# Query and key splits for two heads at once, copied into place by transfers, with weighed blocks evacuated first and projections reordered

## The chip, the cores and the metric

The kernel runs on one core of one Trainium2 chip. The metric is the device time of one execution in microseconds, as the median of several runs.

## What is computed

Two layers of a decoder trunk over 528 positions (16 learned meta tokens and 512 real ones) of width 1024, in float32. Each layer has a mixer and a ConvGLU feed-forward network (FFN), both between two RMS norms. The mixer reads one combined projection of the normed input and feeds three groups, whose outputs are normed by heads, concatenated and projected back:

```python
q, k, v, f_logit, a_val, a_gate, sc_b, sc_c, sc_x = jnp.split(z, idx, axis=-1)
log_f = jax.nn.log_sigmoid((f_logit + b_forget).astype(jnp.float32))
y_attn = forgetting_attention(q.reshape(hs), k.reshape(hs), v.reshape(hs), log_f)
...
a = a_val * jax.nn.sigmoid(a_gate)
a = causal_depthwise_conv(a, a_dw_w) + a_dw_b
a = jax.nn.silu(layer_norm(a, a_ln_g, a_ln_b))
y_conv = jnp.einsum("blc,ce->ble", a, a_pw_w)
y_sc = sc_b * causal_depthwise_conv(sc_c * sc_x, sc_conv_w)
y = jnp.concatenate([y_attn, y_conv, y_sc], axis=-1)
y = jnp.einsum("ble,ed->bld", head_rms_norm(y, head_g), w_out)
return h + rms_norm(y, post_g)
```

The attention has 8 heads of 64. A logit is q·k/8 + F[t] − F[s], causal, with F the running sum of the log forget gates; a softmax over s follows.

## The kernel before

**Layout and precision.** The sequence lies along the free axis (528 positions, two halves of 264), channels on the 128 partitions. Each float32 operand of a large product is split into a high part, rounded to the fast format fp32r, and a low part, the rest; a product is three passes, high·high, high·low, low·high (`mm3`, L639 to L652). So TensorE gets 3 passes x 8 channel blocks x 2 halves = 48 products of 264 columns for each projection of 128 output channels.

**Weights.** A weight block of 128 x 1024 is loaded by SyncE into one of three `raw` buffers (L615), cast to its high part by ScalarE (L619) and its low part taken by VectorE (L623).

**The mixer.** `mixer_steps` lists the projections. Those of the conv module's gate and of the first short-conv group come first; the others run as one thread, `fill`, in the order of the list: v and q, k for pairs of heads (j = 0 to 3), the second short-conv group (sc_c, sc_x, sc_b with j = 1), and `pw`, at which the conv module's tail starts as a thread (`conv_tail`: mean at L1539, variance at L1568, SiLU by Exp and Ln, pointwise product, head norm). Beside `fill` run `maxima`, `exponentials` and `att_norms`.

- `q_proj` and `k_proj` (L1290 and following) project two heads at once into a PSUM bank and split them: for each head and half, ScalarE writes the high part (L1298, L1326) and VectorE the low part (L1303, L1331), 64 partitions each. A head has four tiles, k1, k2, q1 and q2: k1 and q1 hold the high parts on the head's 64 rows and gate and maximum on the other rows; q2 holds q's low part on the other rows and k2 its own low part, and one transfer each (L530, tiles `q<-q` and `k<-k`) copies the high part beside it. There are four such sets of tiles, so heads 4 to 7 reuse those of heads 0 to 3.
- `maxima` (L1372) multiplies q1 by k1 by blocks of queries to find each row's maximum (VectorE, L1379), puts the maxima on a diagonal (GpSimd, L1387) and spreads them by a product (L1396) into a row of q1 (ScalarE, L1398).
- `exponentials` multiplies two pairs of tiles into transposed logits (`logits`, L1416), which ScalarE exponentiates (`pf`, L1423) and GpSimd masks on diagonal blocks (L1430); two blocks later `weigh` multiplies them by the values (L1450) into `acc`, for which there is one PSUM bank. When a query range is summed, ScalarE squares it into `sq` (L1463) and copies it to `yta` (L1464); only then is the bank free.
- `att_norms` norms a pair of heads (L1516) through `head_norm` (L1100 to L1124), which writes `yhi` and `ylo` for the output projection.

When `maxima` and `fill` are over, the output projection of the first half may start on the channel blocks that are normed (`Early`), and on the second half when `exponentials` is over.

**What sets the order.** For ScalarE, VectorE, GpSimd and TensorE, the order is that in which a planner (`Flow`) emits the instructions. Every step is given an engine, a cost in us (`act_us`, `dve_us`, `stt_us`), the tokens that it waits for and a priority; of the steps that are ready, that with the lowest number goes first. Threads (generators) issue TensorE's products and give way to each other where they yield a token. Each engine then runs its instructions in this order. The transfers on SyncE's queue are put in order by the framework, by the tiles that they depend on, and run in that order too.

The gate's rows are spread by ten small transfers (`k<-sq` eight times, `g_dram<-sq` twice, L530), for heads 4 to 7 by two each later (`k<-g_dram`).

## Time and profile before

| | us |
|---|---|
| median of three runs | 1313.34 (1311.2 to 1314.71) |
| the profiled execution | 1311.54 |
| its span, first to last instruction | 1309.8 |
| TensorE busy in the span | 1282.9 |
| VectorE, ScalarE, GpSimd busy | 865.1, 621.2, 97.7 |
| mean granted TensorE clock | 0.996 |

In the profile, PE is TensorE's products, PEld its weight loads, DVE VectorE, ACT ScalarE, POOL GpSimd and SP SyncE; L12 is line 12 of the kernel. A busy PE is not PE at its peak: products are pipelined, and their ends are modelled. A group of instructions is named by its line and by what it writes and reads, `out<-in`. A line of the waits says who waited for whom, with us in total, times, and the longest; in a timeline, a bracket gives the idle time before an instruction and what ended it.

### The profile page before, as it was taken

How to read it: one execution, taken by the hardware profiler on the slowest of the kernel's cores; microseconds unless marked ns; L12 is line 12 of the kernel's file. 1: busy time of each engine (PE TensorE's matmuls, PEld its weight loads, DVE VectorE, ACT ScalarE, POOL GpSimd, SP SyncE). 2: the span in 40 equal slices, each digit the busy share in tenths (PEclk: the TensorE clock that was granted, in tenths of full speed). 3: DMA queues.
4: the chain of work that ended last, by engine and by line, in shares of the span. 5: the costliest groups of instructions: out<-in, count | busy, mean ns of one | idle time of the engine just before them, and what ended most of it. 6: DMA issues, size and time to landing. Idle time of an engine off the chain costs nothing. (4 is left out here: it accounts for less than half of the span.)

```text
span 1309.8 us, 23934 instructions
## 1 busy us (share of the span) xinstructions
PE 1282.9 (98%) x9802; PEld 1228.0 (94%) x9802; DVE 865.1 (66%) x1473; ACT 621.2 (47%) x1167; POOL 97.7 (7%) x254
## 2 busy tenths in 40 slices
PE   8999999999999999999989999999999999999997
PEld 8989898999999999999989898889999799989997
DVE  7888865688634663566676888656876246646664
ACT  7255567564423342344662556675643233314353
POOL 1322311000000000000003223110000000000000
PEclk9999999999999999999989999999999999999999
DMA  6133111602222223223340332125032233233321
GB/s 236 34 99 89 60 58 50 223 20 85 94 95 83 98 72 106 91 85 99 108 137 18 99 90 71 47 74 200 17 97 97 85 94 95 71 110 96 92 71 65
DMA packets 42797, 118.26 MB, mean 90 GB/s; under 512 B 4848, under 2 KB 15216, under 8 KB 42688
## 3 DMA queue, kind: packets, MB, share of 16 engines
q1 hardware_dynamic: 42640, 116.61, 28.0%
q8 instruction: 77, 1.26, 0.4%
q14 instruction: 32, 0.26, 0.1%
q0 software_dynamic: 48, 0.13, 0.0%
HBM read 108.04 MB, written 4.33 MB: 86 GB/s over the span
## 5 line engine op out<-in xcount | busy, mean ns | idle before, releaser
L650 PE MATMUL psum<-uhi,whi 128*128 128x264 f32 (+1 forms) x1936 | 451.5, 287 | 1.9 <-ACT uhi L831 1.1
L650 PE MATMUL psum<-ulo,whi 128*128 128x264 f32 (+1 forms) x1936 | 446.7, 285 | 0.5 <-DVE ulo L1827 0.4
L650 PE MATMUL psum<-uhi,wlo 128*128 128x264 f32 (+1 forms) x1936 | 444.8, 284 | 0.0
L650 PEld LDWEIGHTS psum<-uhi,whi 128*128 128x128 f32 x1936 | 322.9, 189 | 5.8 <-issue 2.4
L650 PEld LDWEIGHTS psum<-ulo,whi 128*128 128x128 f32 x1936 | 323.8, 189 | 1.4 <-DVE ulo L1827 0.6
L650 PEld LDWEIGHTS psum<-uhi,wlo 128*128 128x128 f32 x1936 | 323.7, 189 | 0.0
L650 PE MATMUL psum<-yhi,whi 128*128 128x264 f32 (+3 forms) x888 | 249.6, 304 | 1.5 <-ACT yp L1978 1.0
L650 PE MATMUL psum<-ylo,whi 128*128 128x264 f32 (+3 forms) x888 | 245.6, 299 | 1.0 <-DVE ylo L1124 0.8
L650 PE MATMUL psum<-yhi,wlo 128*128 128x264 f32 (+3 forms) x888 | 245.5, 299 | 1.0 <-DVE wlo L623 0.9
L505 ACT CAST whi<-raw 128x1024 fp32r<-128x1024 f32 (+1 forms) x110 | 113.3, 1031 | 213.0 <-PE psum L650 199.4
L506 DVE TENSOR_TENSOR wlo<-raw,whi 128x1024 fp32r<-128x1024 f32 (+1 forms) x110 | 131.9, 1200 | 81.6 <-ACT whi L505 79.5
L650 PEld LDWEIGHTS psum<-yhi,whi 128*128 128x128 f32 x888 | 159.1, 188 | 10.1 <-ACT yp L1978 1.4
L650 PEld LDWEIGHTS psum<-ylo,whi 128*128 128x128 f32 x888 | 159.3, 188 | 7.6 <-DVE ylo L1124 2.0
L650 PEld LDWEIGHTS psum<-yhi,wlo 128*128 128x128 f32 x888 | 159.1, 188 | 7.2 <-DVE wlo L623 1.8
L1927 DVE SCALAR_TENSOR_TENSOR c<-z,pv,c 128x528 f32<-128x528 f32 (+1 forms) x176 | 132.0, 756 | 2.7
L623 DVE TENSOR_TENSOR wlo<-raw,whi 128x1024 fp32r<-128x1024 f32 (+2 forms) x86 | 102.4, 1205 | 36.6 <-ACT whi L619 35.9
L619 ACT CAST whi<-raw 128x1024 fp32r<-128x1024 f32 (+2 forms) x86 | 87.7, 1033 | 32.4 <-DMA raw<-in_w_dram 17.3
L966 DVE SCALAR_TENSOR_TENSOR cacc<-apad,pv,cacc 128x528 f32<-128x528 f32 x120 | 87.7, 772 | 0.5
L1945 ACT CAST yhi<-c 128x528 fp32r<-128x528 f32 (+1 forms) x44 | 27.6, 627 | 111.3 <-DVE c L1941 111.3
L1937 ACT ACTIVATE c<-c 128x528 f32<-128x528 f32 (+1 forms) x44 | 28.1, 639 | 81.7 <-DVE c L1927 81.7
L1890 DVE TENSOR_TENSOR z<-psum,rz 128x528 f32<-128x528 f32 x40 | 28.3, 708 | 53.8 <-PE psum L650 52.2
L1925 ACT ACTIVATE c<-z,pv 128x528 f32<-128x528 f32 (+1 forms) x88 | 63.3, 726 | 0.0
(212 smaller groups left out, 1438.2 us busy)
## 6 DMA issues: line engine op xcount, KB each, us to landing
raw<-in_w_dram SPq DMA_DIRECT2D x160, 512.0 KB
raw<-in_w_dram SPq DMA_DIRECT2D x32, 448.0 KB
h<-in_x_dram SPq DMA_DIRECT2D x16, 264.0 KB
raw<-in_w_dram SPq DMA_DIRECT2D x4, 528.0 KB
q<-q SPq DMA_DIRECT2D x16, 132.0 KB
k<-k SPq DMA_DIRECT2D x16, 132.0 KB
h_dram<-h SPq DMA_DIRECT2D x4, 528.0 KB
h<-h_dram SPq DMA_DIRECT2D x8, 264.0 KB
```

The source lines that it names most:

```text
L505: nc.scalar.copy(hi[:, :sz], raw[:, :sz])
L506: nc.vector.tensor_sub(lo[:, :sz], raw[:, :sz], hi[:, :sz].bitcast(F32))
L619: nc.scalar.copy(box["hi"][:, :sz], box["raw"][:, :sz])
L623: nc.vector.tensor_sub(lo[:, :sz], box["raw"][:, :sz], box["hi"][:, :sz].bitcast(F32))
L650: nc.tensor.matmul(d, lhsT=w[a][:, k, cols], rhs=rhs(b, k, hf), start=start and i == 0 and p == 0, stop=stop and i == n - 1 and p == 2)
L966: nc.vector.scalar_tensor_tensor(conv[j], in0=src, in1=conv[j], scalar=col("a_dw_w", CK * j + i), op0=ALU.mult, op1=ALU.add)
L1890: nc.vector.tensor_mul(two(t[:, off:]), srcs[0], two(rz))
L1925: nc.scalar.activation(dst, src[:, 2:2 + 2 * fw], AF.Copy, scale=wtap(2, t))
L1927: nc.vector.scalar_tensor_tensor(dst, in0=src[:, i:i + 2 * fw], scalar=wtap(i, t), in1=dst, op0=ALU.mult, op1=ALU.add)
L1937: silu = nc.scalar.activation(cs[0], cs[0], AF.Silu)
L1945: nc.scalar.copy(ghi, cs[0])
```

## The change

There are three parts.

1. `mixer_steps`: `v` with j = 1 goes ahead of the third pair's q and k, `pw` ahead of the fourth pair's; the second short-conv group comes last.
2. `q_proj` and `k_proj`: the high part of both heads is written by one ScalarE step per half, over 128 partitions, into a tile `pair_hi`, and the low part by one VectorE step into `pair_lo` (two buffers each, `NPAIR`). Transfers on SyncE's queue then copy 64 partitions each into the heads' tiles: for q, the high part to q1 and q2 and the low part to q2; for k, the high part to k1 and k2 and the low part to k2. That is three per head and tensor, where there was one. The maxima now wait for transfers of q and k.
3. `weigh`: both evacuations get priority 0 (1 before). The tokens that the square waits for are now those of the last pair's norm product (`norm_mm`) and no longer those of the whole norm (`norm_at`).

```diff
 def mixer_steps():
-    return [("sc_c", 0), ("sc_x", 0), ("v", 0), ("q", 0), ("k", 0), ("sc_b", 0), ("q", 1), ("k", 1), ("q", 2),
-            ("k", 2), ("v", 1), ("q", 3), ("k", 3), ("sc_c", 1), ("pw", 0), ("sc_x", 1), ("sc_b", 1)]
+    return [("sc_c", 0), ("sc_x", 0), ("v", 0), ("q", 0), ("k", 0), ("sc_b", 0), ("q", 1),
+            ("k", 1), ("v", 1), ("q", 2), ("k", 2), ("pw", 0), ("q", 3), ("k", 3), ("sc_c", 1), ("sc_x", 1), ("sc_b", 1)]
...
+            yield from proj(split_pair(j, DH ** -0.5, q_pair))
+            for hd in (2 * j, 2 * j + 1):
                 main, other, _ = rows(hd)
                 q1, q2 = qh[hd % 4]
+                q_at[hd] = [part(q_pair[j], "hi", q1, main, main), *([zeros[hd]] if hd in zeros else [])]
+                q2_at[hd] = [part(q_pair[j], "lo", q2, other, main), part(q_pair[j], "hi", q2, main, main)]
+            q_pair[j]["slot"].close()
+
+        q_pair, k_pair, pair_ring = {}, {}, Ring(NPAIR)
+
+        def part(box, name, t, to, main):
+            tok = flow.op("sp", 0.48, lambda: nc.sync.dma_start(t[to].bitcast(F32), box[name][main].bitcast(F32)),
+                          box[name, "at"], lat=2.2)
+            box["slot"].use(tok)
+            return tok
+
+        def split_pair(j, scale, pairs):
+            box = pairs[j] = {"slot": Slot(), ("hi", "at"): [], ("lo", "at"): []}
             def use(hf, ps, tok):
...
+                    nc.scalar.activation(box["hi"][:, c], ps, AF.Copy, scale=scale)
...
+                    nc.vector.scalar_tensor_tensor(box["lo"][:, c], in0=ps, scalar=scale, in1=box["hi"][:, c].bitcast(F32),
+                                                   op0=ALU.mult, op1=ALU.subtract)
+                a = act(act_us(H), high, tok, *box["hi", "at"], prio=0, takes=() if hf else [(pair_ring, box["slot"])])
+                d = dve(stt_us(H), low, a, prio=0)
...
         def k_proj(j):
...
+            yield from proj(split_pair(j, 1.0, k_pair))
             for hd in (2 * j, 2 * j + 1):
                 main, other, _ = rows(hd)
                 k1, k2 = kh[hd % 4]
-                q2_at[hd].append(dma(k2[other].bitcast(F32), k1[main].bitcast(F32), *k_at[hd], lat=2.2))
+                k_at[hd] = [part(k_pair[j], "hi", k1, main, main)]
+                q2_at[hd] += [k_at[hd][0], part(k_pair[j], "lo", k2, main, main), part(k_pair[j], "hi", k2, other, main)]
...
-                waits = norm_at.get(pr - 1 if e == 0 else None, [zero]) + norm_at.get(pr - 1, [zero])
+                waits = norm_mm.get(pr - 1, [zero])
                 n = qz - qa
-                a = act(act_us(n), lambda: nc.scalar.activation(sq[:, qa:qz], acc[:, :n], AF.Square), tok, *waits)
-                c = act(act_us(n), lambda: nc.scalar.copy(yt[r, qa:qz], acc[r, :n]), tok)
+                a = act(act_us(n), lambda: nc.scalar.activation(sq[:, qa:qz], acc[:, :n], AF.Square), tok, *waits, prio=0)
+                c = act(act_us(n), lambda: nc.scalar.copy(yt[r, qa:qz], acc[r, :n]), tok, prio=0)
```

More of the change, by code (lines that the diff above doesn't have):

```diff
@@ L50 @@
 NP = 6
+NPAIR = 2
 WARM, WARM_US = 44, 8.0
@@ L1294, in q_proj @@
                      for hd in (2 * j, 2 * j + 1)} if j > 1 else {}
-            def high(hd, c, ps):
-                main = rows(hd)[0]
-                nc.scalar.activation(qh[hd % 4][0][main, c], ps[main], AF.Copy, scale=DH ** -0.5)
-            def low(hd, c, ps):
+            yield from proj(split_pair(j, DH ** -0.5, q_pair))
+            for hd in (2 * j, 2 * j + 1):
                 main, other, _ = rows(hd)
                 q1, q2 = qh[hd % 4]
-                nc.vector.scalar_tensor_tensor(q2[other, c], in0=ps[main], scalar=DH ** -0.5,
-                                               in1=q1[main, c].bitcast(F32), op0=ALU.mult, op1=ALU.subtract)
@@ L1306, in use @@
-            def use(hf, ps, tok):
-                out = []
-                for hd in (2 * j, 2 * j + 1):
-                    c = half_sl(hf)
-                    a = act(act_us(H), lambda hd=hd: high(hd, c, ps), tok, prio=0)
-                    d = dve(dve_us(H), lambda hd=hd: low(hd, c, ps), a, prio=0)
-                    q_at.setdefault(hd, [zeros[hd]] if hd in zeros else []).append(a)
-                    q2_at.setdefault(hd, []).append(d)
-                    out += [a, d]
-                return out
@@ L1317, in q_proj @@
-            yield from proj(use)
-            for hd in (2 * j, 2 * j + 1):
-                main = rows(hd)[0]
-                q1, q2 = qh[hd % 4]
-                q2_at[hd].append(dma(q2[main].bitcast(F32), q1[main].bitcast(F32), *q_at[hd], lat=2.2))
-        def k_proj(j):
-            def high(hd, c, ps):
-                main = rows(hd)[0]
-                nc.scalar.copy(kh[hd % 4][0][main, c], ps[main])
-            def low(hd, c, ps):
-                main = rows(hd)[0]
-                k1, k2 = kh[hd % 4]
-                nc.vector.tensor_sub(k2[main, c], ps[main], k1[main, c].bitcast(F32))
-            def use(hf, ps, tok):
-                out = []
-                for hd in (2 * j, 2 * j + 1):
-                    c = half_sl(hf)
-                    a = act(act_us(H), lambda hd=hd: high(hd, c, ps), tok, prio=0)
-                    d = dve(dve_us(H), lambda hd=hd: low(hd, c, ps), a, prio=0)
-                    q2_at[hd] += [a, d]
-                    if hf == 0:
-                        k_at[hd, 0] = a
-                    else:
-                        k_at[hd] = [k_at[hd, 0], a]
-                    out += [a, d]
-                return out
-            yield from proj(use)
@@ new lines, in split_pair, with high, low @@
+        def split_pair(j, scale, pairs):
+            box = pairs[j] = {"slot": Slot(), ("hi", "at"): [], ("lo", "at"): []}
+            def use(hf, ps, tok):
+                c = half_sl(hf)
+                def high():
+                    if hf == 0:
+                        box["hi"], box["lo"] = (T(ap, [P, L], F32R, f"pair_{n}", NPAIR) for n in ("hi", "lo"))
+                    nc.scalar.activation(box["hi"][:, c], ps, AF.Copy, scale=scale)
+                def low():
+                    nc.vector.scalar_tensor_tensor(box["lo"][:, c], in0=ps, scalar=scale, in1=box["hi"][:, c].bitcast(F32),
+                                                   op0=ALU.mult, op1=ALU.subtract)
+                a = act(act_us(H), high, tok, *box["hi", "at"], prio=0, takes=() if hf else [(pair_ring, box["slot"])])
+                d = dve(stt_us(H), low, a, prio=0)
+                box["hi", "at"].append(a)
+                box["lo", "at"].append(d)
+                return [a, d]
+            return use
@@ L1350, in k_proj @@
                 k1, k2 = kh[hd % 4]
-                q2_at[hd].append(dma(k2[other].bitcast(F32), k1[main].bitcast(F32), *k_at[hd], lat=2.2))
+                k_at[hd] = [part(k_pair[j], "hi", k1, main, main)]
+                q2_at[hd] += [k_at[hd][0], part(k_pair[j], "lo", k2, main, main), part(k_pair[j], "hi", k2, other, main)]
                 if j > 1:
                     gate_rows(hd, *g_done)
+            k_pair[j]["slot"].close()
             k2_at[j] = True
```

## The prediction

> **What bounds the kernel now.** I began with the page: which engine is busy, and whether any other comes near it. Then one table of stages, to see where TensorE stands still; then the waits of its weight loads, the first thing of a product to be held up; then single stretches.

> ```profile
> span 1309.8 us, 23934 instructions
> PE 1282.9 (98%) x9802; PEld 1228.0 (94%) x9802; DVE 865.1 (66%) x1473; ACT 621.2 (47%) x1167; POOL 97.7 (7%) x254
> ```

> ```profile
> core 0: us, PE busy (x) PEld busy (x) DVE busy (x) ACT busy (x) POOL busy (x), PEclk, DMA share, GB/s
> 60.00:100.00 40.00, 38.75 (x294) 35.90 (x293) 35.82 (x85) 20.01 (x51) 7.15 (x16) 1.00 0.29 82
> 180.00:220.00 40.00, 37.81 (x262) 33.30 (x261) 25.91 (x67) 32.79 (x92) 6.09 (x19) 1.00 0.12 41
> 350.00:400.00 50.00, 50.00 (x412) 50.00 (x411) 17.88 (x20) 14.72 (x20) 0.00 (x0) 1.00 0.28 96
> 840.00:880.00 40.00, 37.25 (x261) 32.57 (x260) 26.04 (x59) 33.74 (x94) 3.75 (x9) 1.00 0.10 29
> ```

> TensorE is busy 98% of the span, and the change adds or removes no product, so it can only win time in which TensorE waits. The table says where: in the FFN (350 to 400) it never stops, and 50 us / 412 gives 0.121 us for one projection product of 264 columns. The mixers run from about 45 to 230 and from 695 to 885. Their ends (180 to 220, 840 to 880) lose 2.2 and 2.75 us of 40, and there ScalarE is at its fullest, 32.8 and 33.7 us of 40. The waits of the weight loads name the culprits:

> ```profile
> PEld psum L1450 <- POOL pf L1430: 5.6, 8, 1.4
> ...
> PEld psum L1450 <- ACT sq L1463: 2.2, 2, 1.1
> PEld psum L650 <- DVE ylo L1124: 2.0, 5, 0.5
> PEld psum L650 <- DVE wlo L623: 1.8, 4, 0.6
> ...
> PEld psum L1264 <- DVE gt L1256: 1.8, 2, 0.9
> ...
> PEld psum L650 <- ACT yhi L1123: 0.9, 4, 0.3
> ```

> The columns are us in total, times, longest. The weighing product (L1450, weights times values) waits 5.6 + 2.2 = 7.8 us in the two layers, 3.9 us in each. The first products of the output projection wait for their normed input (L1123 and L1124) 2.0 + 0.9 = 2.9 us, and for weight pieces (L623) 1.8. The forget gate's 1.8 (L1264) isn't touched. All that the change can reach is thus 7.8 + 2.9 + 1.8 = 12.5 us, 1.0% of the span. This caps the gain.

> What do the two longest waits look like? ScalarE, GpSimd and TensorE late in the first mixer:

> ```profile
> 195.73 0.72 ACT L1560 CAST yhi<-cacc 128x264 fp32r<-128x264 f32 x2
> 196.34 0.43 ACT L1557 ACTIVATE apad<-apad 128x264 f32<-128x264 f32 x1
> 196.67 0.27 ACT L1463 ACTIVATE sq<-psum 128x128 f32<-128x128 f32 x1
> 196.82 0.42 ACT L1557 ACTIVATE apad<-apad 128x264 f32<-128x264 f32 x1
> 197.14 1.04 ACT L619 CAST whi<-raw 128x1024 fp32r<-128x1024 f32 x1
> ```

> ```profile
> 198.74 1.75 POOL L1430 TENSOR_SCALAR_AFFINE_SELECT pf<-pf 128x128 f32<-128x128 f32 x2 [7.97 <-ACT pf L1423]
> ```

> ```profile
> 196.99 0.94 PE L1450 MATMUL psum<-pf,vals 128*128 128x400 f32 x2 [0.92 <-ACT sq L1463]
> 200.29 0.50 PE L1450 MATMUL psum<-pf,vals 128*128 128x272 f32 x1 [1.27 <-POOL pf L1430]
> ```

> One PSUM bank holds the weighed block. Its evacuation (sq) stood behind the conv module's steps (apad, yhi) on ScalarE, and the next weighing waited 0.92 us. Then a weight cast of 1.04 us went ahead of an exponential, and the weighing that needs its masked block waited 1.27. And TensorE had nothing else to do: in the built order of instructions, 11 of the 48 weighings of a mixer stand behind its last projection product.

> **The change part by part.**

> *Order of the projections and evacuation at priority 0.* In the built order of the changed kernel no weighing stands behind the last projection product (0 of 48, against 11), and the conv module's mean (L1539 before) moves from behind head 5 to behind head 3, so that its Exp and Ln steps are over when the last heads are weighed. Between two neighbouring weighings there are now mostly 3 to 9 projection products, 0.4 to 1.1 us, where before some had 39 to 72 and those at the end none. The evacuation of a block also has fewer tokens to wait for in the plan (the last norm's product instead of its whole chain), which can only let it go earlier. So I take 3.1 of the 3.9 us as gone in each mixer and 0.8 as left, since a cover of 3 products (0.36 us) is thin beside one late ScalarE step (0.43). Bounds: all 3.9 stays, all goes. **2 x -3.1 = -6.2 us.**

> *End of a mixer.* Before, the two conv norms and the last attention norm run there together; after, the conv norms are done and the second short-conv norm takes their place, with 51 products (6.2 us) between its mean and its first use. Of the 2.9 us of waits at L1123 and L1124 I take 2.2 as gone. Bounds 0 and 2.9; the 1.8 us for weight pieces I leave as they are, bounds 0 and 1.8. **-2.2 us.**

> *Splits of two heads at once.* The durations, min/median/max:

> ```profile
> L1298 ACT ACTIVATE q<-psum x32: 364/386/388, 68.3 to 812.7; 64x264 fp32r<-64x264 f32 x32
> L1303 DVE SCALAR_TENSOR_TENSOR q<-psum,q x32: 425/431/435, 69.7 to 813.5; 64x264 fp32r<-64x264 f32 x32
> L530 SPq DMA_DIRECT2D q<-q x16: 462/496/1980, 70.6 to 813.2; - x16
> ```

> ```profile
> 85.38 0.42 ACT L1130 ACTIVATE cxp<-sccx 128x264 f32<-128x264 f32 x1
> ```

> ```profile
> 82.29 0.43 DVE L1044 TENSOR_TENSOR sccx<-psum,sccx 128x264 f32<-128x264 f32 x1
> ```

> A layer has 8 query and key projections. Each had 4 ScalarE and 4 VectorE steps on 64 partitions and gets 2 and 2 on 128. ScalarE: 32 x 0.386 = 12.4 against 16 x 0.42 = 6.7, so 5.6 us less per layer; VectorE: 32 x 0.431 = 13.8 against 16 x 0.43 = 6.9, so 6.9 less. Worth nothing by itself: TensorE's products cover both engines, and a PSUM bank that comes free earlier was waited for nowhere above. Its effect is in the 3.1 already counted. The copies go to the queue of SyncE: 3 per head for q and 3 for k, 48 per layer where 16 were, 32 x 0.50 = 16 us more of issuing in a stage of 180 us. The queue holds weight loads too, but they are issued ahead and wait there for a free buffer; I take 0, and what it costs without that cover is in the third rival.

> *The new wait.* Before, the maxima (L1372) read q and k that ScalarE wrote itself. Now they need a transfer, and the first one stands in the queue behind the gate's ten:

> ```profile
> 74.89 5.00 SPq L530 DMA_DIRECT2D k<-sq  x8
> 79.94 0.84 SPq L530 DMA_DIRECT2D g_dram<-sq  x2
> 80.88 1.43 SPq L530 DMA_DIRECT2D k<-k  x2
> ```

> ```profile
> L1372 PE MATMUL psum<-k,q x96: 170/294/458, 78.9 to 836.9; 128*128 128x264 f32 x32, 128*16 128x16 f32 x16, 128*128 128x144 f32 x16, 128*128 128x272 f32 x16
> L1416 PE MATMUL psum<-q,k x192: 170/344/601, 85.9 to 866.1; 128*128 128x400 f32 x64, 128*128 128x128 f32 x32, 128*128 128x272 f32 x32, 128*128 128x144 f32 x32
> ```

> The built order has 24 more projection products ahead of the first maximum (3 fewer before the gate, 27 more behind it): TensorE arrives at 78.9 + 24 x 0.121 = 81.8. The transfer of k's high part can't be issued before about 80.9, where k<-k was. No row gives its landing. It lies above its own issue, 0.5 us. From above: the opening's first h load follows a weight load and releases ScalarE 4.6 us after its issue at 1.72:

> ```profile
> 1.26 0.42 SPq L615 DMA_DIRECT2D raw<-in_w_dram  x1
> 1.72 1.98 SPq L462 DMA_DIRECT2D h<-in_x_dram  x4
> ```

> ```profile
> 6.30 0.93 ACT L1801 ACTIVATE yhi<-h,pg 128x264 fp32r<-128x264 f32 x2 [4.22 <-DMA h<-in_x_dram]
> ```

> The nearer row is k<-k itself: the logits, which need it, start unhindered at 85.9, so it takes at most 5.0 us from 80.9. I take 2.3, somewhat under the middle of 0.5 and 4.6, as no weight load stands right ahead: landing at 83.2, a wait of **1.4 us per mixer, +2.8**; bounds 0 and 80.9 + 4.6 - 81.8 = 3.7 each. Behind the waiting product the projections queue on TensorE; nothing else suffers. At the next three pairs the built order leaves 3.7, 4.8 and 5.0 us of products between k's last product and the first maximum; ScalarE 0.42, issue 0.5 and the rest of 2.3 fit in, so 0.

> **Sum:** -6.2 - 2.2 + 2.8 = -5.6 us. The profiled execution took 1311.54 us (span 1309.8); the median of the three runs is 1313.34, 1.8 above. So 1305.9 on the profiled one's scale, **1307.7 us** on the median's.

> **The rivals.**

> *Given back.* The waits move rather than go: evenly spread heads have 3 products of cover almost everywhere, and each ScalarE step that comes late costs a bit at many weighings. Half of 7.8 stays, the end gains nothing: -3.9 + 2.8 = -1.1, 1312.2 us. For it: the thin covers. Against: ScalarE has 20 of 40 us busy at 60 to 100, where few long waits are, and loses 5.6 us more of work per layer.

> *Transfers behind weight loads (slower).* The queue is in order and already stands waiting for TensorE:

> ```profile
> SPq L530 <- PE psum L1416: 36.1, 8, 7.0
> ```

> If at each pair a load of 512 KB goes just ahead, the landing takes 4.6 us: 3.7 us at the first pair, and at the others 0.42 + 0.5 + 4.6 = 5.5 against 3.7, 4.8 and 5.0, so 1.8 + 0.7 + 0.5 = 3.0. Per mixer 6.7, together 13.4 - 6.2 - 2.2 = +5.0: 1318.3 us. It decides from a landing of 3.9 us on: then the first two pairs' waits, 3.0 + 1.2, use up the 4.2 us that a mixer gains. Against: the built order puts a load directly ahead of k's transfers at two pairs of four only, the second and the third, and there it can be issued while k is still being multiplied.

> *The clock.* Right after layer 0 TensorE's granted clock fell:

> ```profile
> 655.00:660.00 5.00, 2.75 (x11) 1.59 (x9) 4.15 (x8) 3.70 (x8) 0.00 (x0) 0.82 0.68 243
> 660.00:665.00 5.00, 3.78 (x15) 3.48 (x16) 4.24 (x8) 4.99 (x10) 0.00 (x0) 0.50 0.00 0
> ```

> That is 5 x 0.18 + 5 x 0.50 = 3.4 us of full clock lost, after 2.25 us without products; waits of 1.3 us in the mixers left it at 1.00. Whether a gap is punished may hang on its moment, which the change shifts by some us: without the stretch -5.6 - 3.4 = -9.0, 1304.3 us; with another one in a mixer, where the new wait comes near 3.7 us, 1311.1. [...]

> **How the numbers follow.** The forecast gets 0.48, given back 0.24, slow transfers 0.17, the clock falling away 0.11. The range reaches from 1302 (forecast with all of 12.5 gone but the new wait, 1313.3 - 12.5 + 2.8 = 1303.6, and a little of the clock) to 1319 (slow transfers and 0.7 more). By itself the forecast would have 1304 to 1312. A measurement of this kernel tells about 0.3%, 3.9 us, from no change, so faster means below 1309.4: three quarters of the forecast, all of the clock case and a little of the second, 0.36 + 0.11 + 0.03 = 0.50; slower, above 1317.3: most of slow transfers, some of given back, 0.20; within: 0.30.

> **What would show it.** Right: the waits of L1450's successor for GpSimd and ScalarE fall from 7.8 us to about 1.6; a new row, the maxima waiting for a DMA, about 1.4 us once in each mixer; TensorE's busy share at 180 to 220 and 840 to 880 above 39 of 40. Wrong: DMA waits at four pairs of a mixer; or the weighings' waits as before, at other heads; or a second stretch at half clock.

## The result, and the profile after

The changed kernel takes **1322.35 us** (median of four runs, 1321.94 to 1324.02) against 1313.8 for the kernel before: ratio 1.0071, 95% interval 1.0053 to 1.0088. That is 8.55 us slower, where 5.6 us faster was forecast, and above the range. The profiled execution took 1322.66 us, 11.1 more than the one before. In one kernel below, one run of ten (1385.68 us at a granted clock of 0.849) fell into a slower state and is left out of the median. The page and the stages of the kernel after:

```profile
span 1320.9 us, 23912 instructions
PE 1284.8 (97%) x9802; PEld 1232.3 (93%) x9802; DVE 849.0 (64%) x1441; ACT 608.9 (46%) x1135; POOL 99.4 (8%) x254
```

```profile
60.00:100.00 40.00, 34.50 (x253) 32.49 (x252) 30.67 (x74) 14.20 (x33) 4.95 (x11) 0.91 0.45 109
180.00:220.00 40.00, 38.61 (x272) 33.48 (x271) 25.17 (x65) 29.70 (x81) 11.35 (x25) 1.00 0.26 74
840.00:880.00 40.00, 38.60 (x276) 33.77 (x275) 26.20 (x70) 30.17 (x81) 11.06 (x24) 1.00 0.22 64
```

The ends of the mixers gained, as forecast (37.81 and 37.25 us busy before). The loss is at 60 to 100: TensorE is busy 34.50 us of 40 where it was 38.75, and its granted clock is 0.91. The waits of TensorE's products and, in the last line, of its weight loads. Where nothing else is said, a wait below is that of products; the weight load ahead of a product waits about 0.2 us longer.

```profile
PE psum L1366 <- DMA k<-pair_hi: 13.3, 4, 4.8
...
PE psum L651 <- DVE pair_lo L1327: 1.5, 4, 0.6
PE psum L1390 <- POOL cxp L1017: 1.4, 2, 0.7
...
PE psum L651 <- DVE rs_t L1106: 0.6, 2, 0.3
...
PE psum L1410 <- ACT q L1392: 0.5, 2, 0.3
```

```profile
PEld psum L1444 <- POOL pf L1424: 0.2, 1, 0.2
```

By the weight loads, the weighing (now L1444) waits 0.2 us, 7.8 before: that gain came. But the maxima (L1366) wait 13.3 us for k's transfers, four times: at the first and the second pair of each mixer (4.8 and 1.7 us, 4.3 and 2.5 us). The four rows of short waits, 4.0 us in all, are new too. SyncE's queue around the first of the four waits for k, which ends at 86.9:

```profile
71.03 0.53 SPq L1309 DMA_DIRECT2D q<-pair_hi  x1
71.65 0.53 SPq L616 DMA_DIRECT2D raw<-in_w_dram  x1
72.23 1.75 SPq L1309 DMA_DIRECT2D q<-pair_hi  x3
74.02 1.29 SPq L1309 DMA_DIRECT2D q<-pair_lo  x2
75.41 0.54 SPq L616 DMA_DIRECT2D raw<-in_w_dram  x1
76.06 7.52 SPq L531 DMA_DIRECT2D k<-sq  x8
...
84.56 2.42 SPq L1309 DMA_DIRECT2D k<-pair_hi  x4
```

The gate's eight small transfers took 7.52 us where they took 5.00, and began 1.2 us later; k's first transfer went out at 84.56, not at 80.9 (where `k<-k` was before). Next, the granted clock, by stretches of 3.41 us:

```profile
81.49:84.90 3.41, 0.61 (x6) 0.40 (x4) 1.04 (x2) 0.42 (x1) 0.00 (x0) 1.00 0.14 38
84.90:88.32 3.42, 1.43 (x7) 1.46 (x8) 0.49 (x4) 0.00 (x0) 0.64 (x2) 0.50 0.75 164
88.32:91.73 3.41, 3.41 (x17) 3.41 (x16) 1.17 (x5) 0.00 (x0) 0.71 (x2) 0.50 0.62 141
115.62:119.04 3.42, 2.36 (x21) 2.16 (x19) 2.26 (x3) 0.58 (x2) 0.00 (x0) 1.00 0.83 259
740.26:743.68 3.42, 0.39 (x4) 0.42 (x5) 0.17 (x2) 0.00 (x0) 0.00 (x0) 1.00 0.55 119
743.68:747.09 3.41, 3.41 (x17) 3.41 (x17) 1.05 (x5) 0.00 (x0) 1.01 (x3) 0.50 0.94 252
774.40:777.81 3.41, 1.55 (x13) 1.59 (x14) 0.78 (x5) 0.00 (x0) 0.64 (x2) 1.00 1.09 238
777.81:781.22 3.41, 3.41 (x18) 3.40 (x17) 1.93 (x9) 0.38 (x1) 0.89 (x3) 0.50 0.28 83
```

Behind three of the four waits the clock falls to one half; the second pair's in the first mixer (the stretch from 115.62) leaves it up. In these stretches products keep TensorE busy for 1.43 + 3.41 + 3.41 + 3.41 = 11.7 us, which at the full clock would be 5.8 us less. For the ledger, the waits of the products before that are gone now:

```profile
PE psum L1450 <- POOL pf L1430: 4.1, 6, 1.3
...
PE psum L1450 <- ACT sq L1463: 1.8, 2, 0.9
PE psum L1264 <- DVE gt L1256: 1.4, 2, 0.7
...
PE psum L650 <- DVE ylo L1124: 0.8, 3, 0.3
```

TensorE is not busy for 1320.9 - 1284.8 = 36.1 us, 9.2 more than the 26.9 before: 13.3 + 4.0 new, 8.1 gone. Its busy time grew by 1.9: 5.8 for the clock, less 3.9 of other busy time, whose cause I can't name.

### The profile page after: what moved, and what is told of

Its sections match the earlier page's. It is cut to its first block, busy times and chain, and to the rows that moved or that the text cites. A ratio compares the mean times of both kernels' runs of the same rounds, so it can differ in the third digit from the quotient of the medians.

```text
span 1320.9 us, 23912 instructions
## 1 busy us (share of the span) xinstructions
PE 1284.8 (97%) x9802; PEld 1232.3 (93%) x9802; DVE 849.0 (64%) x1441; ACT 608.9 (46%) x1135; POOL 99.4 (8%) x254
## 3 DMA queue, kind: packets, MB, share of 16 engines
q8 instruction: 77, 1.26, 0.4%
## 5 line engine op out<-in xcount | busy, mean ns | idle before, releaser
L507 DVE TENSOR_TENSOR wlo<-raw,whi 128x1024 fp32r<-128x1024 f32 (+1 forms) x110 | 132.0, 1201 | 82.1 <-ACT whi L506 80.0
L1931 ACT ACTIVATE c<-c 128x528 f32<-128x528 f32 (+1 forms) x44 | 28.1, 640 | 81.8 <-DVE c L1921 81.8
```

The costliest lines, as they stand in the source:

```text
L507: nc.vector.tensor_sub(lo[:, :sz], raw[:, :sz], hi[:, :sz].bitcast(F32))
L1931: silu = nc.scalar.activation(cs[0], cs[0], AF.Silu)
```

## The experiments

Times are medians with the kernel before measured on the same chip beside them (1312.78 us for the first four; 1312.27 for the three with k written directly and the one with the plan corrected; 1311.95 for the two with the gate on GpSimd's queue; 1311.8 for the two at the end with the first pair's q, or its q and k, as before). My theory after the result was: the loss is the wait for k's transfer and the half clock behind it; order, evacuation and lighter split gain as forecast.

**Order and evacuation alone.** The kernel before with the new `mixer_steps` and the new `weigh`:

```diff
-            ("k", 2), ("v", 1), ("q", 3), ("k", 3), ("sc_c", 1), ("pw", 0), ("sc_x", 1), ("sc_b", 1)]
+            ("k", 1), ("v", 1), ("q", 2), ("k", 2), ("pw", 0), ("q", 3), ("k", 3), ("sc_c", 1), ("sc_x", 1), ("sc_b", 1)]
...
+                waits = norm_mm.get(pr - 1, [zero])
```

> The kernel before with the new order of the projections and the evacuation at priority 0, but with the old split (each head's parts written straight into its tiles). Theory (the maxima's wait for transfers, and the half clock that follows it, outweigh a gain of the order that is there): the weighing's 7.8 us and about 2 of the 2.9 us at the end go, nothing is added: about 1303 to 1305 us, the weighing's waits (L1450) near 0.2 us. Rival (the order itself moves the waits): 1312 us or more, with new waits of 0.2 to 0.5 us at many weighings.

Measured: 1314.55 us, ratio 1.0012 (1.0002 to 1.0023). My theory missed. Its waits of TensorE:

```profile
PE psum L650 <- DVE wlo L623: 2.3, 4, 0.8
PE psum L650 <- DVE q L1303: 1.9, 2, 0.9
...
PE psum L1372 <- DVE mcol L1379: 1.4, 3, 0.9
...
PE psum L1568 <- DVE q L1303: 1.4, 2, 1.2
...
PE psum L1450 <- POOL pf L1430: 0.9, 2, 0.5
```

The weighing's waits for a masked block fell from 4.1 to 0.9 us, but VectorE now comes late with the old split itself (q, L1303, 3.3 us), with weights (2.3) and maxima (1.4). In the changed kernel, which has the same order, the rows for the split, the weights and the maxima are 1.5, 0.7 and 0.3 us. So the order needs VectorE's lighter split (849.0 us of work instead of 865.0); I had taken that split to be worth nothing.

**The split alone.** The changed kernel with the old order, priority and tokens:

```diff
-            ("k", 1), ("v", 1), ("q", 2), ("k", 2), ("pw", 0), ("q", 3), ("k", 3), ("sc_c", 1), ("sc_x", 1), ("sc_b", 1)]
+            ("k", 2), ("v", 1), ("q", 3), ("k", 3), ("sc_c", 1), ("pw", 0), ("sc_x", 1), ("sc_b", 1)]
...
-                waits = norm_mm.get(pr - 1, [zero])
```

> The kernel after with the old order of projections, the old priority and the old tokens of the evacuation: the split by pairs and its transfers alone. Theory: the first maximum of each mixer waits 4 to 5 us for the transfer of k, a later pair's 2 us, the clock falls to one half behind these waits for 3 to 7 us; with the weighing's waits kept the time is 1328 to 1334 us. Rival (the transfers cost little, the order costs): 1313 to 1317 us.

Measured: 1327.59 us, ratio 1.0114 (1.0076 to 1.0152). That is 0.4 us under what I expected, and far from the rival. The wait for k and the weighing's wait are both there, and one more:

```profile
PE psum L1366 <- DMA k<-pair_hi: 4.8, 1, 4.8
PE psum L1137 <- ACT cacc L1577: 4.8, 2, 2.4
PE psum L1444 <- ACT sq L1457: 3.7, 2, 1.9
```

The maxima's wait in the second mixer is 2.3 us, and no later pair waits. The clock weighs more than I thought: in six stretches of the mixers, four of them at the mixers' ends behind the other two rows, products run for 22.6 us at half clock, which is 11.3 us lost. By medians the two parts alone cost 1.8 and 14.8 us and together 8.6, so they don't add. The order gains beside the split (though the intervals of 1.0071 and 1.0114 overlap) and not without it; the split costs in both cases here, as long as TensorE waits for its transfers.

**What does the clock cost?** Products without use keep TensorE at work until k's transfer lands:

```diff
                         s = s[:n, :z - a]
+                        for _ in range({0: 36, 2: 14}.get(hd, 0) if b == 0 else 0):
+                            nc.tensor.matmul(s[:, :H], lhsT=ones_r, rhs=uhi[:, 0, :H], start=True, stop=True)
```

> The kernel after, with 36 products of 264 columns into the bank of the first maximum ahead of it in each mixer, and 14 ahead of the third head's: they are overwritten by the real product and fill the time that TensorE waits for the transfer (36 x 0.121 = 4.4 us, 14 x 0.121 = 1.7 us), and nothing else changes. It measures the clock alone. Theory (half clock costs 2.4 us behind the wait in the first mixer and 1.7 + 1.7 in the second): the clock stays at 1.00 in the mixers and the time falls by about 5.8 us, to 1316 to 1318. Rival (the half clock lies in time that is waited out anyway): 1321 to 1324 us, as after.

Measured: 1317.23 us, ratio 1.0032 (1.0022 to 1.0042), with the clock at full speed throughout the mixers:

```profile
PE psum L1368 <- DMA k<-pair_hi: 0.6, 1, 0.6
```

The hundred added products take 100 x 0.121 = 12.1 us, about the time that was waited before, and still the kernel is 5.1 us faster than the changed one: the half clock costs some 5 us.

**Fewer small transfers ahead of k.** The gate's rows of heads 2 and 3 come later, from `g_dram`, so four small transfers stand ahead of k's first instead of eight:

```diff
-            for hd in range(4):
+            for hd in range(2):
...
-                if j > 1:
+                if j > 0:
```

> The kernel after, with the gate's rows of heads 2 and 3 sent later, by way of DRAM as those of heads 4 to 7: four small transfers instead of eight stand ahead of k's first transfer on SyncE's queue. Theory (the first wait is the queue, at about 0.7 to 0.9 us for each small transfer): k's first transfer is issued 2.8 to 3.8 us earlier, the first maximum waits 1 to 1.6 us instead of 4.8 and 4.4, and the clock stays up there: 1311 to 1314 us. Rival (the wait is the landing of the transfer itself, not the queue): 1321 to 1324 us.

Measured: 1313.19 us, ratio 1.0003 (0.999 to 1.0017). The time is a hit, the way to it only in part: k's first transfer went out 2.4 us earlier (82.18), the first pair waits 3.0 and 1.4 us, and the clock still fell in both mixers:

```profile
PE psum L1366 <- DMA k<-pair_hi: 7.1, 4, 3.0
```

**No transfer in the path of the maxima.** k of the first two pairs, or of the first alone, is split as before (`k_alone` is the old `k_proj`); in the third kernel the second pair's k goes out on GpSimd's queue as well:

```diff
         def k_proj(j):
+            if j < 2:
+                yield from k_alone(j)
+                return
             yield from proj(split_pair(j, 1.0, k_pair))
```

> The changed kernel, but k of the first two pairs is split as before (ScalarE and VectorE write 64 partitions each straight into the heads' tiles, one transfer each for the copy), so the first maximum of these pairs needs no transfer of k; everything else is as changed. Theory (the loss is the wait for k's transfer at the first two pairs, 13.3 us, and the half clock that follows it, some 5 us; the rest of the change gains about 9): no row of the maxima waiting for k's transfer, no half clock in the mixers, 1304 to 1308 us. Rival (the transfers cost in other places too, the spread order only moves waits): the waits come back at the weighings or logits, 1311 us or more.

> The same for the first pair's k alone; the second pair's k still goes by transfers behind a weight load. Theory (the two pairs' waits have two causes: the gate's eight small transfers at the first, the weight load at the second): the wait at the second pair stays, 1.5 to 3 us in each mixer, with none to 3.4 us of half clock, 1308 to 1313 us. Rival (the second pair's wait only follows from the delay at the first): no wait left, 1304 to 1308 us.

> As the kernel with the first pair's k direct, and the second pair's high parts of k for the maxima are issued on GpSimd's queue, past SyncE's with its weight load. Theory (the transfer lands late because it stands in one queue behind the load): the wait at the second pair falls under 1 us in each mixer, 1304 to 1309 us. Rival (the load and the transfer share the 16 DMA engines, whatever the queue): the wait stays at 1.5 to 3 us, as with the first pair direct, 1308 to 1313 us.

Measured: 1319.74 us (ratio 1.0047, 1.0032 to 1.0062), 1316.53 (1.0028, 1.0014 to 1.0042), 1318.67 (1.0042, 1.0025 to 1.0059). All three missed. Each has the same row; here that of the first:

```profile
PE psum L1402 <- DMA k<-sq: 9.4, 2, 4.7
```

TensorE now comes to the first maximum at 79.0 us and waits until 83.6 for the gate's rows. Thus the culprit wasn't k's transfer alone: the gate's rows, issued ahead of it, land late too. What is left ahead of them is q's six transfers and weight loads. The wait at the second pair vanished in the second kernel, as its rival had it: there the weight load goes out 2.0 us ahead of k's transfer (114.24 and 116.22), and no maximum waits for that. In the changed kernel the load is 0.45 us ahead, and by the landing records of the trace (16 for each such transfer, the last of which I take) the transfer needs 4.0 us, where the first pair's, at 84.56, needed 2.2:

```profile
115.07 0.36 SPq L616 DMA_DIRECT2D raw<-in_w_dram  x1
115.52 2.39 SPq L1309 DMA_DIRECT2D k<-pair_hi  x4
```

The kernel with GpSimd's queue (0.6 and 0.4 us of wait there) thus told nothing about queues, since its partner had no wait left to take away.

**Is it the queue?** In the built order each transfer on SyncE's queue waits for the eighth before it to land (eight semaphores in turn). The records agree: the second of the gate's transfers goes out at 78.29, just when the weight load of 71.65, eight places ahead, is down (78.22). So I moved the gate's eight small transfers to GpSimd's queue, and in a second kernel also told the planner of the second pair's late landing:

```diff
+                if hd < 4:
+                    gate_at[hd].append(gp(0.55, lambda to=to, src=src: nc.gpsimd.dma_start(to, src), *after, lat=2.0))
```

> The changed kernel, with the gate's eight small transfers for heads 0 to 3 issued on GpSimd's queue; TensorE's order ahead of the first maximum stays. Theory (each transfer on SyncE's queue waits until the eighth before it has landed, so with q's six transfers and a weight load just ahead the gate's small ones become slow, and k's stand behind them): k's first transfer goes out by 80 us where it went at 84.56, the wait of the first pair's maximum falls from 4.9 and 4.5 us to under 1.5 each, and no half clock follows it; what is left is the second pair's wait, 1305 to 1313 us. Rival (k's transfer lands late because the DMA engines are full of weight loads, whatever stands ahead on the queue): the first pair still waits 3 us or more in each mixer, 1316 us or more.

> The same, and the planner is told that the second pair's high part of k lands 5.2 us after its split (2.2 assumed before); the first pair's stays at 2.2. Theory: no wait of the maxima for a transfer above 1.5 us at either pair, clock full in the mixers, 1303 to 1308 us, about the kernel whose plan alone was corrected (1307.57) or below it. Rival (GpSimd's issues or later landing of the gate's rows cost as much as they win): 1308 us or more, with a new wait for the gate's rows or for GpSimd.

Measured: 1320.5 us (ratio 1.0054, 1.0035 to 1.0073; its ten runs lie between 1311.55 and 1323.94) and 1316.23 (1.0024, 1.0012 to 1.0036). My theory fell with both. The rival held for the first kernel; for the second only its time did, since what is left is again the wait for k, not one for the gate's rows or GpSimd. From the first kernel, the queue, then the wait, then the last line on the gate's transfers, min, median and max from issue to landing:

```profile
79.02 3.01 SPq L1313 DMA_DIRECT2D k<-pair_hi  x4
```

```profile
PE psum L1370 <- DMA k<-pair_hi: 13.7, 4, 5.2
```

```profile
DMA to landing us min/median/max: 7.4/8.2/8.4
```

k's transfer goes out 5.5 us earlier than in the changed kernel and lands at the same time, 86.8 in both: the DMA engines themselves are behind. The next to last column of the stages, their busy share, says so. First the changed kernel, then this one:

```profile
72.00:76.00 4.00, 3.96 (x31) 3.55 (x32) 4.00 (x8) 1.03 (x3) 0.00 (x0) 1.00 0.95 243
76.00:80.00 4.00, 4.00 (x35) 4.00 (x34) 3.71 (x8) 1.33 (x2) 0.00 (x0) 1.00 1.09 204
80.00:84.00 4.00, 2.10 (x18) 1.89 (x16) 2.29 (x4) 0.42 (x1) 0.00 (x0) 1.00 0.36 70
```

```profile
80.00:84.00 4.00, 1.91 (x16) 1.70 (x15) 2.10 (x3) 0.42 (x1) 0.00 (x0) 1.00 1.01 185
```

Full from 72 to 80, at 204 to 243 GB/s: q's six copies (0.8 MB) beside three weight loads (1.5 MB). In the changed kernel they have little to do from 82 on (a share of 0.10 up to 84), while the queue, held up by those late landings, still issues the gate's transfers. With GpSimd's queue they stay full until 84, as k's copies join the rest earlier, and even the first of these needs 7.8 us to land. In the second kernel 8.9 us of waiting were left, all at the first pair.

**Fewer copies of q.** q of the first pair is split as before, with two copies instead of six; k goes by transfers as changed:

```diff
+            if j == 0:
+                yield from q_alone(j, zeros)
+                return
             yield from proj(split_pair(j, DH ** -0.5, q_pair))
```

> The changed kernel, but q of the first pair is split as before (two copying transfers of 132 KB instead of six); k of all pairs by transfers, TensorE's order ahead of the first maximum the same. Theory (q's four additional transfers, 0.5 MB, keep the DMA engines full until 82 us, so everything issued behind lands late, whatever its queue): the DMA share at 76 to 80 falls from over 1.0 to about 0.3 as before, k's first transfer goes out at 81 to 82 us instead of 84.56 and lands 2.3 us later, the first pair's maximum waits 1 to 2.5 us in each mixer instead of 4.9 and 4.5; 1307 to 1315 us. Rival (eight small transfers of the gate ahead are slow by themselves): the wait stays at 3.5 us or more, 1317 us or more.

Measured: 1313.25 us, ratio 1.0009 (1.0 to 1.0018), as the theory said; the share at 76 to 80 fell to 0.48, not to 0.3. DMA share, queue and wait:

```profile
76.00:80.00 4.00, 4.00 (x35) 4.00 (x34) 4.00 (x9) 1.21 (x3) 0.00 (x0) 1.00 0.48 137
```

```profile
75.74 4.99 SPq L531 DMA_DIRECT2D k<-sq  x8
...
81.72 2.44 SPq L1340 DMA_DIRECT2D k<-pair_hi  x4
```

```profile
PE psum L1397 <- DMA k<-pair_hi: 7.1, 4, 2.2
```

The gate's transfers take 4.99 us again, k's goes out at 81.72, and the first pair waits 1.4 us in each mixer: what I had forecast for the changed kernel. The second pair waits 2.1 and 2.2 behind its weight load. The clock stays full in the mixers. The copies are not the only difference, since the first pair's q also has its old steps on ScalarE and VectorE; but the queue, the engines' share and the wait moved together as the theory has it.

**Two ways to win.** Either the transfers stay and the planner is told when k is there (`lat`), or the first pair is split as before (q and k) and the planner told of the second:

```diff
-                k_at[hd] = [part(k_pair[j], "hi", k1, main, main)]
+                k_at[hd] = [part(k_pair[j], "hi", k1, main, main, {0: 7.4, 1: 5.2}.get(j, 2.2))]
```

> The changed kernel with all its transfers; only the planner is told when k's high part is there: 7.4 us after the split at the first pair and 5.2 at the second, where it assumes 2.2. TensorE gets projection products ahead of the first maximum in place of a wait. Theory (the loss is a wait that the plan did not foresee, not the transfers): the row of the maxima waiting for k's transfer falls under 3 us in all, no half clock in the mixers, 1304 to 1309 us. Rival (the products that cover the wait are missing later, at the weighings): these waits come back with 3 to 6 us, 1310 us or more.

> Both q and k of the first pair are split as before, the other three pairs by transfers as changed; the planner is told that the second pair's k lands 5.2 us after its split. Theory (the loss is in the first pair's transfers ahead of and in the first maximum, and in the second pair's late one): no wait of a maximum for a transfer above 1 us, clock full in the mixers, and with the gains of the order and of the lighter split kept 1302 to 1307 us. Rival (what the lighter split and the order gain hangs on the late first maximum, as more projections were left behind it): 1309 us or more, with waits at the weighings or the logits.

Measured: 1307.57 us (ratio 0.9958, 0.9943 to 0.9972) and **1307.47 us** (0.9968, 0.9955 to 0.998), both faster than either kernel. The first is in the range of its theory, the second 0.5 us above. No maximum waits for a transfer, and the clock is full in the mixers. The first one's page and waits:

```profile
span 1305.4 us, 23918 instructions
PE 1280.4 (98%) x9802; PEld 1226.0 (94%) x9802; DVE 847.9 (65%) x1441; ACT 609.6 (47%) x1135; POOL 101.3 (8%) x254
```

```profile
PE psum L1366 <- DVE mcol L1373: 1.7, 5, 0.4
PE psum L1390 <- POOL cxp L1017: 1.4, 2, 0.7
...
PE psum L651 <- DVE pair_lo L1327: 1.1, 2, 0.6
```

Its transfers go out when those of the changed kernel did, k's at 84.17; TensorE multiplies projections meanwhile. Short waits for VectorE and GpSimd have come in, and TensorE is not busy for 25.0 us, only 1.9 less than the 26.9 before. The other 2.5 of the 4.4 us that the span lost are busy time (1282.9 before).

## Why the prediction was wrong, point by point

The profiled execution ended 16.7 us above the forecast (11.1 more instead of 5.6 less): 10.5 for the waits for k (13.3 instead of 2.8), 5.8 for the half clock and 4.0 for new short waits; the waits that went gave 8.1 instead of 8.4; the 3.9 of other busy time go off.

- **Waits of the weighing, -6.2:** right, and somewhat small. By the weight loads, the 7.8 us became 0.2. But it is no gain of the order alone, as the first experiment shows; it needs VectorE's lighter split, which I had costed at nothing beyond it.
- **End of a mixer, -2.2:** the waits at L1123 and L1124 are gone (2.9 us by the weight loads), but at the same ends products now wait for a norm's start (rs_t), for GpSimd's conv steps (cxp) and for the spread maxima (q), 2.5 us in their place, so nearly nothing was gained there. TensorE is busy for 38.6 of 40 us at both ends, short of the 39 that I asked for.
- **The new wait, +2.8: the step that failed.** TensorE's arrival (81.8, measured 82.1) was right, and the landing after the issue, 2.2 us against my 2.3. Wrong was the issue: "can't be issued before about 80.9, where k<-k was" was a lower bound, and I used it as the time. I had counted q's and k's copies as 16 us more of issuing on a queue, "I take 0", and not as bytes: 0.5 MB more ahead of the first maximum, on engines whose share at 76 to 80 was 0.32 before (below) and is 1.09 now. Without these four copies the wait was 1.4 us in each mixer, as forecast.

```profile
76.00:80.00 4.00, 4.00 (x34) 3.99 (x33) 3.41 (x9) 1.78 (x4) 0.17 (x1) 1.00 0.32 115
```

- **The next three pairs, 0:** wrong at the second: its landing of 4.0 us behind a weight load (5.4 in the second mixer) left 1.7 and 2.5 us of wait. Right at the third and fourth.
- **Rival "transfers behind weight loads":** its price, 13.4 us, was that measured (13.3) by chance only: 4.8 and 4.3 at the first pair, not 3.7, and by q's copies rather than a load right ahead; 1.7 and 2.5 at the second, where a load does stand right ahead; nothing at the third and fourth.
- **Rival "the clock":** another stretch came at three places and cost 5.1 us, and the one after layer 0 stayed (665.17 to 672.00). I had kept it apart from the slow transfers, though it came behind the waits for them (4.8, 4.3 and 2.5 us, not 1.7): together 1318.3 + 5.1 = 1323.4, where 1322.35 was measured. The two should have been one case.
- **Given back:** true in its direction. With all waits for transfers gone, the kernel gains 4.3 to 4.7 us and not 8.4, and less than half of that is waiting.
- **"It can only win time in which TensorE waits":** not so. Without half of the busy time at half clock in the mixers, TensorE is busy for 1282.9 us before, 1281.7 with the order alone, 1279.3 with the split alone, 1279.0 in the changed kernel and 1280.4 with the plan corrected. So most of what busy time lost goes with the split; by what means, no run here settles. The forget gate's wait (L1264, 1.8 us by the weight loads), said to be untouched, went too; it is back in the kernels with the first pair's q as before.

## What to carry to other kernels

When a change replaces an engine's own write by transfers, count their bytes on the DMA engines in the stretch just ahead of the first use, not only their issues on a queue; here, where the engines' share at 76 to 80 was 1.09, the gate's 2 KB transfers took up to 7.2 us to land when issued on SyncE's queue, and 7.4 to 8.4 on GpSimd's. If a hand-made plan orders the work, give it the landing that the trace shows; here that alone turned 0.7% slower into 0.4% faster. And price a wait on TensorE with the half clock that it may bring: here 5.1 us in all, behind three waits of four.
